# Query tiles in pairs and one written sequence, from the last linear head to the end

## Chip, cores, metric

One core of one Trainium2 chip runs the whole program in one launch. The metric is device time in microseconds (us). A kernel's time is the median of its runs.

## What is computed

One transformer block over 512 tokens of width 1024, all in float32. A wide input projection feeds two mixers: four heads of gated linear attention, in both directions, and eight heads of ordinary attention with low-rank queries and keys (64 plain and 32 rotated dimensions a head, values of 128). The two are mixed by sigmoid gates, projected by `w_out`, and an MLP of width 4096 follows.

```python
def mla_branch(cq, ckv, kr, positions, g_q, w_uq, g_kv, w_ukv):
    q = (rmsnorm(cq, g_q) @ w_uq).reshape(B, S, H, MLA_QK_HEAD)
    ...
    def attend(qblk):
        s = jnp.einsum('bhqd,bhkd->bhqk', qblk, kt).astype(jnp.float32)
        p = jax.nn.softmax(s, axis=-1)
        return jnp.einsum('bhqk,bhkv->bhqv', p.astype(vt.dtype), vt)
...
    merged = jax.nn.sigmoid(z_ma) * y_gla + jax.nn.sigmoid(z_mb) * y_mla
    h = h + merged @ w_out[l]
    m = rmsnorm(h, g_mlp[l])
    h = h + jnp.square(jax.nn.relu(m @ w_ff1[l])) @ w_ff2[l]
    return rmsnorm(h, g_final)
```

## The kernel before

**Products.** A float32 product is made of three matmuls in the chip's rounded format (fp32r): every operand is split into a high part and a low remainder, and `mm3` (L87 to L90) multiplies high by high, high by low, low by high. So behind each value that TensorE makes stand two more operations: a copy on ScalarE that rounds it (the tile whose name ends in `h`, L93) and a subtraction that keeps the remainder (`l`, L94), on VectorE or GpSimd. Transpositions go through TensorE in plain float32.

**Stages, by the time of the trace.** The input projection and most of the linear heads fill the time to about 255 us. From 255 to 290 us the last linear head (h = 3) is computed among the first queries and keys of the attention. From 290 to 374 us the attention's eight heads run, each over four tiles of 128 queries; from 374 to 413 us the output projection (a product of quarters in the manner of Strassen, `wox`, `wow`, `woz` being its banks); then four pairs of MLP phases to 722 us, whose steps are set by a table of due times, and `last_rows`, which norms and stores the last rows.

**The attention's loop (L1369 to L1453).** One turn of the loop scores one query tile: `att_scores` multiplies queries by keys (`s`, one PSUM bank), VectorE takes the row's maximum (`top`), ScalarE the exponential and its sum (`e`). Every second turn `att_normalise` divides two tiles by their sums, one on ScalarE and one on VectorE. Three turns later `att_flip` transposes one tile's four key blocks into a bank (`tp`) and splits them (`pT`). Six turns later `att_values` multiplies values by two flipped tiles, so that a head's values are two runs of twelve matmuls 256 columns wide (`av`). `merge` gates the result (`tb` on VectorE, `mx` and `my` on GpSimd, L1153). The sums of quarters `yo` and `zo`, the splits `gao`, `ghyo`, `glyo`, and the loads for `w_out` are strewn between the turns. GpSimd also issues the transfers that add their source onto a tile that is already loaded (L980, L1626; the loaded tiles are called `w`, in the orders `w2_..`).

**What sets the order.** A scheduler places the instructions of TensorE, ScalarE and VectorE in this stretch, held at some points by `goes_behind` (one instruction after another on the same engine). `in_program_order` fixes an engine to the order in which the code is written: GpSimd from the attention on, the other compute engines from the output projection on, SyncE (which issues the plain loads) from the MLP's steps on. An engine takes its instructions in the order of its queue.

**The end.** `last_rows` (L1745) sums the last products into rows 2 and 3 of tokens: `out_mean` (L1717) and `out_gained` (L1720, the gain times the row) on GpSimd, `out_square` on ScalarE, the two halves of row 3 added on VectorE (L1754, `gend0` and `gend1`), `out_rstd` (a power, L1730) on GpSimd, then one scaled product for each half of a row (L1734 on VectorE, L1738 on ScalarE) and the store.

Of the kernel before, what the change touches and what calls it, by code (L numbers as in the profile page):

```python
# [18 lines left out]
P = 128  # L19
# [35 lines left out]

@with_exitstack
def tile_block(ctx: ExitStack, tc: tile.TileContext, t, out: bass.AP):
    nc = tc.nc
# [76 lines left out]
    make_identity(nc, ident)  # L135
# [887 lines left out]
    def up_units(pr):  # L1023
# [29 lines left out]
        qs = [u4(f"q{pr}{i}") for i in range(2)]  # L1053
# [5 lines left out]
        if apart:  # L1059
            for i in range(2):  # L1060
                split_scaled(qs[i][0:64, 0, :], qs[i][0:64, 1, :], accq[i * 64 : i * 64 + 64, :], QK_SCALE)
        else:
            split_scaled(qs[0][:, 0, :], qs[0][:, 1, :], accq, QK_SCALE)
            nc.sync.dma_start(raw(qs[1][0:64]), raw(qs[0][64:128]))
            rotary_rows(0)
# [29 lines left out]
    def att_scores(head, qt):  # L1095
# [4 lines left out]
        mm3(acc, q[d, 0, tok], q[d, 1, tok], kb[d, 0, :], kb[d, 1, :], True, True)  # L1100
        top = sm("top", 1)
        nc.vector.tensor_reduce(top, acc, axis=AX.X, op=ALU.max, negate=True)  # L1102
        e = u2(f"e{head}{qt}")
        if qt % 2 == 0:
            tots[head] = sm("tot", 2)
# [10 lines left out]
    def att_flip(head, qt):  # L1116
        e = probs.pop((head, qt))
        if qt % 2 == 0:
            pTs[head, qt // 2] = [u4(f"pT{head}{qt}{x}", F32R, (P, NT, 256)) for x in range(2)]
        tp = ps("at", f"tp{head}{qt}")  # L1120
        for k in range(NT):
            nc.tensor.transpose(tp[:, k * P : (k + 1) * P], e[:, k * P : (k + 1) * P], ident)  # L1122
        hi, lo = pTs[head, qt // 2]
        c = slice((qt % 2) * P, (qt % 2 + 1) * P)
        split(hi[:, :, c], lo[:, :, c], tp.rearrange("p (k q) -> p k q", k=NT))

    def att_values(head, half):
        if half == 0:
            avs[head] = ps("mm", f"av{head}")
        acc = avs[head]  # L1130
        hi, lo = pTs.pop((head, half))
        _, _, vs, c = heads[head]
        for k in range(NT):
# [3 lines left out]
        if head < MH - 1:  # L1137
            if half == 1:
                merge(head, acc, (0, 1))
        else:  # L1140
            merge(head, acc, (half,))
# [167 lines left out]

    h = GH - 1  # L1310
# [27 lines left out]
    first_units = traced()  # L1338
# [3 lines left out]
    first_units = first_units, traced()  # L1342
    at = traced()
    zb = proj_run(w_b, xT)
    last_gate = at, traced()
    g2.append(gated(zb, "b7")[1])
    in_program_order(fixed, SPLITTERS)
    in_program_order(ordered, PE_ONLY)
    in_program_order(pooled, (mybir.EngineType.Pool,))
# [14 lines left out]
    at = traced()  # L1364
    next(units)
    goes_behind((at, traced()), first_units, SPLITTERS[:1])
    attending = traced()
    sums_of, flipping, span = {}, {}, {}
    for n in range(4 * MH + LAG_C - 1):  # L1369
        if n % 2 == 0 and 2 <= n <= 4 * MH:  # L1370
            att_normalise((n - 2) // 4, (n - 2) % 4)
        scored = traced()
        if n < 4 * MH:
            att_scores(n // 4, n % 4)
            if n - 2 in flipping:
                goes_behind((scored, traced()), flipping[n - 2], SPLITTERS)
        scored = scored, traced()
        if n == 0:
            goes_behind(scored, last_gate, PE_ONLY)
        if n == 3:  # L1380
            span["fourth"] = scored
        if 2 <= n % 8 < 7:
            at = traced()
# [3 lines left out]
            if n < 4:  # L1387
                goes_behind((at, traced()), scored, PE_ONLY)
        if n in (6, 14):
            units = up_units(n // 8 + 2)  # L1390
            at = traced()
            next(units)
            if n == 6:
                goes_behind((at, traced()), span["fourth"], SPLITTERS[:1])
        b = n - LAG_B
        if n == 30:
            xs_ = wo_accs[1] = [ps("mm", f"wox{rb}") for rb in range(2)]
            at = traced()
            wo_product(1, ps_=(0,))
            begun = at, traced()  # L1400
            goes_behind(begun, scored, PE_ONLY)
        if 0 <= b < 4 * MH:
            flips = traced()
            att_flip(b // 4, b % 4)
            flipping[n] = flips, traced()
            if n == 30:
                goes_behind(flipping[n], begun, PE_ONLY)

        if n == 20:
            load_onto(B11, B12, w_out)  # L1410
        extra = traced()
# [8 lines left out]
        if n < 4 * MH:  # L1420
            goes_behind((extra, traced()), scored, SPLITTERS[:1])
# [7 lines left out]
        if n == 17:  # L1429
            at = traced()  # L1430
            load_wo(B21, B22)
            span["sums"] = at, traced()
# [6 lines left out]
        if c >= 0 and c % 2 == 1:  # L1439
            valued = traced()  # L1440
            att_values(c // 4, (c % 4) // 2)
            valued = valued, traced()
        if n == 35:
            at = traced()
            split_first(wo_left[2], merged[2][0], "o2")
            goes_behind((at, traced()), valued, SPLITTERS[1:])
# [298 lines left out]
    def last_rows(ph):  # L1745

        begun = traced()
# [10 lines left out]
        for i in (2, 3):  # L1758
            out_first(i)
        out_gained(2)  # L1760
        out_mean(2)
# [8 lines left out]
        out_mean(3)  # L1770
# [3 lines left out]
        out_store(1)  # L1774
        p = hparts[3]
        nc.vector.scalar_tensor_tensor(p[:, 2:3], p[:, 1:2], 1.0 / D, p[:, 2:3], op0=ALU.mult, op1=ALU.add)
        last_part(1)
# [8 lines left out]
        in_program_order(begun)  # L1786

    begun = traced()  # L1790
# [8 lines left out]
    att_values(MH - 1, 1)  # L1799
# [8 lines left out]
    at = traced()  # L1808
# [190 lines left out]
```

## Time and profile before

| | |
|---|---|
| median of 3 runs | 738.93 us (738.71 to 739.01) |
| the profiled run | 739.02 us |
| its span in the trace | 737.3 us |
| granted TensorE clock | 0.998 of full speed |
| matmuls and transpositions | 4226 |
| VectorE instructions | 861 |
| ScalarE instructions | 809 |
| GpSimd instructions | 284 |

The span is what the trace covers from the first to the last instruction; 1.72 us of the run lie outside it. Busy shares are means over the whole span, so the stretch that the change touches is read from windows of 20 us. Matmuls overlap, so the cost of one is the distance from its start to the next one's start, not its length in the trace.

### The profile page before, as it was taken

How to read it: one execution, taken by the hardware profiler on the slowest of the kernel's cores; microseconds unless marked ns; L12 is line 12 of the kernel's file. 1: busy time of each engine (PE TensorE's matmuls, PEld its weight loads, DVE VectorE, ACT ScalarE, POOL GpSimd, SP SyncE). 2: the span in 40 equal slices, each digit the busy share in tenths (PEclk: the TensorE clock that was granted, in tenths of full speed). 3: DMA queues.
4: the chain of work that ended last, by engine and by line, in shares of the span. 5: the costliest groups of instructions: out<-in, count | busy, mean ns of one | idle time of the engine just before them, and what ended most of it. 6: DMA issues, size and time to landing. Idle time of an engine off the chain costs nothing.

```text
span 737.3 us, 11473 instructions
## 1 busy us (share of the span) xinstructions
PE 726.9 (99%) x4226; PEld 643.1 (87%) x4226; DVE 625.0 (85%) x861; ACT 494.2 (67%) x809; POOL 220.7 (30%) x284
## 2 busy tenths in 40 slices
PE   9999999999999999999999999999999999999995
PEld 7888888888888888899888899889988998899984
DVE  7777787889988788798898889998699869987896
ACT  7557465595696675988856879545874477537764
POOL 0732020243743724126852511200211012101215
PEclk9999999999999999999999999999999999999999
DMA  9849682431222324557978899862987088815773
GB/s 309 277 100 215 215 188 90 79 64 31 58 58 58 51 72 89 127 111 214 291 145 233 133 267 185 184 204 63 250 181 192 20 240 175 196 57 146 170 114 114
DMA packets 80520, 109.95 MB, mean 149 GB/s; under 512 B 15920, under 2 KB 34352, under 8 KB 80464
## 3 DMA queue, kind: packets, MB, share of 16 engines
q1 hardware_dynamic: 63088, 75.64, 32.9%
q0 software_dynamic: 17088, 33.30, 27.1%
q8 instruction: 33, 0.54, 0.3%
q10 hardware_dynamic: 288, 0.28, 0.1%
q14 instruction: 23, 0.19, 0.1%
HBM read 104.22 MB, written 2.10 MB: 144 GB/s over the span
## 4 chain that ended last, share of the span: by engine, by line
PE 88%; DVE 5%; issue 2%; POOL 2%; ACT 1%; DMA 1%; POOLq 0%; DVEq 0%; ACTq 0%
PE first L326 3%; PE tp L1122 2%; PE zb L88 1%; PE zb L89 1%; PE zb L90 1%; PE f2x L90 1%; PE f3x L90 1%; PE f1x L90 1%; PE f3x L89 1%; PE f2x L89 1%; PE f1x L89 1%; PE f1x L88 1%; PE f3x L88 1%; PE f2x L88 1%; PE av L89 1%
## 5 line engine op out<-in xcount | busy, mean ns | idle before, releaser
L1626 POOL DMA_DIRECT2D w<-in_w_ff x40 | 48.3, 1240 | 254.9 <-DMA w<-in_w_ff 139.3
L1102 DVE TENSOR_REDUCE top<-s 128x1 f32<-128x512 f32 x32 | 21.6, 682 | 4.9 <-PE s L90 4.7
L1107 ACT ACTIVATE e<-s,top 128x512 f32<-128x512 f32 x32 | 21.9, 687 | 3.5 <-DVE top L1102 2.6
L94 DVE TENSOR_TENSOR pT<-tp,pT 128x512 fp32r<-128x512 f32 x32 | 21.8, 682 | 2.4 <-ACT pT L93 2.0
L93 ACT ACTIVATE pT<-tp 128x512 fp32r<-128x512 f32 x32 | 19.0, 595 | 3.2 <-PE tp L1122 3.2
L1122 PE MATMUL tp<-ident,e 128*128 128x128 f32 x128 | 19.4, 274 | 0.0
L88 PE MATMUL av<-pT,v 128*128 128x256 f32 x64 | 19.1, 299 | 0.0
L90 PE MATMUL av<-pT,v 128*128 128x256 f32 x64 | 18.2, 285 | 0.0
L89 PE MATMUL av<-pT,v 128*128 128x256 f32 x64 | 18.1, 284 | 0.0
L1122 PEld LDWEIGHTS tp<-ident,e 128*128 128x128 f32 x128 | 15.2, 140 | 3.1 <-ACT e L1113 0.7
L94 POOL TENSOR_TENSOR qF<-qk,qF 128x512 fp32r<-128x512 f32 x4 | 6.6, 1641 | 37.6 <-ACT qF L93 37.6
L667 POOL DMA_DIRECT2D gvw<-in_w_in x4 | 4.8, 1230 | 38.7 <-DVE gvw L672 34.0
L667 POOL DMA_DIRECT2D zaw<-in_w_in x4 | 4.9, 1228 | 32.7 <-DVE zaw L672 28.0
L1628 DVE TENSOR_TENSOR w<-w,w 128x1024 f32<-128x1024 f32 x12 | 14.4, 1220 | 0.1
L980 POOL DMA_DIRECT2D w<-in_w_out x10 | 12.2, 1400 | 6.5 <-DVE bo60l L94 5.3
L88 PE MATMUL s<-kbuf,q 96*128 96x512 f32 x32 | 14.1, 439 | 0.0
L1153 POOL TENSOR_TENSOR mx<-tb,yg 128x256 f32<-128x256 f32 x8 | 7.7, 964 | 19.8 <-DVE tb L1150 13.9
L577 ACT ACTIVATE bds<-bd 128x512 f32<-128x512 f32 x4 | 2.4, 597 | 15.8 <-PE bd L555 15.8
L89 PE MATMUL s<-kbuf,q 96*128 96x512 f32 x32 | 12.6, 395 | 0.0
L90 PE MATMUL s<-kbuf,q 96*128 96x512 f32 x32 | 12.6, 393 | 0.0
L1113 ACT ACTIVATE e<-e,tot 128x512 f32<-128x512 f32 x16 | 11.6, 726 | 1.3 <-DVE tot L1112 1.3
L89 PEld LDWEIGHTS av<-pT,v 128*128 128x128 f32 x64 | 12.2, 191 | 0.2
(2156 smaller groups left out, 3250.4 us busy)
## 6 DMA issues: line engine op xcount, KB each, us to landing
w<-in_w_ff SPq DMA_DIRECT2D x48, 512.0 KB, 5.6
w<-in_w_ff POOLq DMA_DIRECT2D x40, 512.0 KB, 6.2
w<-in_w_out POOLq DMA_DIRECT2D x10, 512.0 KB, 8.3
grw<-in_w_in SPq DMA_DIRECT2D x8, 512.0 KB, 8.6
zaw<-in_w_in SPq DMA_DIRECT2D x8, 512.0 KB, 7.4
gvw<-in_w_in SPq DMA_DIRECT2D x8, 512.0 KB, 4.7
w<-in_w_out SPq DMA_DIRECT2D x16, 256.0 KB, 5.6
w220f<-in_w_ff SPq DMA_DIRECT2D x8, 512.0 KB, 6.2
```

The costliest lines, as they stand in the source:

```text
L88: nc.tensor.matmul(acc, lh, rh, start=start, stop=False, skip_group_check=onto)
L89: nc.tensor.matmul(acc, lh, rl, start=False, stop=False, skip_group_check=onto)
L90: nc.tensor.matmul(acc, ll, rh, start=False, stop=stop, skip_group_check=onto)
L93: nc.scalar.activation(hi, src, AF.Copy)
L94: rest.tensor_tensor(lo, src, raw(hi), op=ALU.subtract)
L326: nc.tensor.matmul(f_accs[i], a[:, i * P : (i + 1) * P], b, start=k == 0 and x == 0, stop=k == KD - 1 and x == 2)
L980: nc.gpsimd.dma_start(d, rows.rearrange("(k t p) w -> p t k w", t=2, p=P)[:, x // 2], accum_op=ALU.add)
L1102: nc.vector.tensor_reduce(top, acc, axis=AX.X, op=ALU.max, negate=True)
L1107: nc.scalar.activation(e, acc, AF.Exp, bias=top, accum_out=tot[:, qt % 2 : qt % 2 + 1])
L1122: nc.tensor.transpose(tp[:, k * P : (k + 1) * P], e[:, k * P : (k + 1) * P], ident)
L1626: nc.gpsimd.dma_start(d, self.source(src, g), accum_op=ALU.add)
L1628: nc.vector.tensor_tensor(d, d, self.tiles(src)[g], op=ALU.add)
```

## The change

**One written sequence.** `nc` is wrapped. From `nc.hold()` on, ahead of the last linear head's scores, every call on an engine is put aside under the engine's letter (P TensorE, A ScalarE, D VectorE, G GpSimd, S SyncE) and the name of the tile that it writes. `nc.emit(SEQUENCE)`, behind the output projection, issues them in the order of a string. Then `in_program_order(written)` fixes all five engines to it, through the MLP to the end. The `goes_behind` calls are gone. In the orders of the changed kernel all these instructions therefore have the wrapper's line, L76, or L90 behind it, and the tile's name tells them apart.

**Query tiles in pairs.** `att_flip` takes two query tiles at once and two key blocks of each, so that a bank holds two key blocks by 256 queries, and `pT` holds all 512 queries of a head. `att_values` runs once for a head over 512 columns (head 7 keeps two halves of 256). Queries are kept as two tiles, high and low, so each transfer of rotated rows (`ro` to `q`) becomes two of half the size.

**Last rows.** GpSimd takes both means ahead of row 2's gain, and VectorE adds `gend1` ahead of the mean term of row 3.

```diff
+    def emit(self, sequence):
+        held, self.held = self.held, None
+        for entry in sequence.split():
+            name, _, count = entry.partition("*")
+            for _ in range(int(count or 1)):
+                what, args, options = held[name].pop(0)
+                what(*args, **options)
...
-                nc.sync.dma_start(raw(qs[i][at : at + HALF]), raw(ro[x][h : h + HALF]))
+                for y in range(2):
+                    nc.sync.dma_start(raw(qs[i][y][at : at + HALF]), raw(ro[x][h : h + HALF, y]))
...
-    def att_flip(head, qt):
-        e = probs.pop((head, qt))
...
+    def att_flip(head, half):
+        if half == 0:
+            pTs[head] = [[u4(f"pT{head}{x}{k}") for k in range(2)] for x in range(2)]
+        es = [probs.pop((head, 2 * half + i)) for i in range(2)]
+        cols = slice(half * HT, (half + 1) * HT)
+        for g, (hi, lo) in enumerate(zip(*pTs[head])):
+            tp = ps("at", f"tp{head}{half}{g}")
+            for i, e in enumerate(es):
+                for k in range(2):
+                    at = k * HT + i * P
+                    nc.tensor.transpose(tp[:, at : at + P], e[:, (2 * g + k) * P : (2 * g + k + 1) * P], ident)
+            split(hi[:, :, cols], lo[:, :, cols], tp.rearrange("p (k q) -> p k q", k=2))
...
-            mm3(acc[:, half * 256 : (half + 1) * 256], vt[:, 0, k % 2, c], vt[:, 1, k % 2, c],
-                hi[:, k, :], lo[:, k, :], k == 0, k == NT - 1)
+            mm3(avs[head][:, cols], vt[:, 0, k % 2, c], vt[:, 1, k % 2, c],
+                his[k // 2][:, k % 2, cols], los[k // 2][:, k % 2, cols], k == 0, k == NT - 1)
...
-        if c >= 0 and c % 2 == 1:
-            valued = traced()
-            att_values(c // 4, (c % 4) // 2)
+        if c >= 0 and (c % 4 == 3 or c == 4 * MH - 3):
+            att_values(c // 4, (0, 1) if c // 4 < MH - 1 else (0,))
...
+    nc.hold()
+    written = traced()
     h = GH - 1
...
+        out_mean(2)
+        out_mean(3)
         out_gained(2)
-        out_mean(2)
...
-        out_mean(3)
         out_gained(3)
...
+        last_part(1)
         p = hparts[3]
         nc.vector.scalar_tensor_tensor(p[:, 2:3], p[:, 1:2], 1.0 / D, p[:, 2:3], op0=ALU.mult, op1=ALU.add)
-        last_part(1)
...
+    SEQUENCE = """
+        S:wr0f*2 S:zb6f S:wr0f A:sin A:qF D:cqc2 S:wr1f A:wr0h A:zb6h G:wr0l P:y15*4 P:y14*4 S:wq0f P:ckvss*4
...
+    nc.emit(SEQUENCE)
...
-    in_program_order(begun, PE_ONLY + SPLITTERS)
-    in_program_order(stepped, SP_ONLY)
-    in_program_order(attending, (mybir.EngineType.Pool,))
     last_rows(g3)
+    in_program_order(written)
```

Three places show how the orders stand. The first is TensorE at the values of head 3, in the middle of the attention. Before, its second half (`pT320` and `pT321` are the high and the low part of query tiles 2 and 3, `v10` the values) comes behind one transposition:

```order
L1122 MATMUL tp42_766_3710<-ident_61,e42_735_3571 128x128 x4
L88 MATMUL av3_749_3630<-pT320_726_3530,v10_612_3071 128x256
L89 MATMUL av3_749_3630<-pT321_727_3531,v10_612_3071 128x256
L90 MATMUL av3_749_3630<-pT320_726_3530,v10_612_3071 128x256
L88 MATMUL av3_749_3630<-pT320_726_3530,v10_612_3071 128x256
L89 MATMUL av3_749_3630<-pT321_727_3531,v10_612_3071 128x256
L90 MATMUL av3_749_3630<-pT320_726_3530,v10_612_3071 128x256
L88 MATMUL av3_749_3630<-pT320_726_3530,v11_618_3102 128x256
```

After, the same stretch reads (`pT300` and `pT310` are now the high and the low part of two key blocks for all 512 queries):

```order
L76 MATMUL tp400_764_2789<-ident_61,e40_724_2749 128x128 x2
L76 MATMUL tp400_764_2789<-ident_61,e41_734_2759 128x128 x2
L76 MATMUL av3_776_2801<-pT300_726_2751,v10_613_2638 128x512
L76 MATMUL av3_776_2801<-pT310_728_2753,v10_613_2638 128x512
L76 MATMUL av3_776_2801<-pT300_726_2751,v10_613_2638 128x512 x2
L76 MATMUL av3_776_2801<-pT310_728_2753,v10_613_2638 128x512
L76 MATMUL av3_776_2801<-pT300_726_2751,v10_613_2638 128x512
L76 MATMUL av3_776_2801<-pT301_727_2752,v11_624_2649 128x512
```

A head has one run of twelve wide matmuls where it had two runs of twelve narrow ones, and the transpositions of a bank take two tiles each.

The second place is GpSimd and ScalarE at the split of `mx1`, the first two query tiles' merged columns of heads 2 and 3 (`gao1`). GpSimd before, up to the remainder of that split:

```order
L1153 TENSOR_TENSOR mx2_802_3859<-tb5_535_2687,yg5_529_2674 128x256
L1153 TENSOR_TENSOR my2_803_3860<-tb5_535_2687,yg5_529_2674 128x256
L1006 TENSOR_TENSOR yo2_831_3972<-my2_803_3860 128x256
L1007 TENSOR_TENSOR yo2_831_3972<-yo2_831_3972,mx2_802_3859 128x256
L1008 TENSOR_TENSOR zo2_832_3973<-mx2_802_3859,my2_803_3860 128x256
L1009 TENSOR_TENSOR zo2_832_3973<-mx2_802_3859,yo2_831_3972 128x256
L94 TENSOR_TENSOR gao1_840_4005<-mx1_731_3557,gao1_840_4005 128x512
```

and after, up to the sum on which that split waits (`DMA w2_..` are adding transfers of `w_out`):

```order
L76 TENSOR_TENSOR my1_739_2764<-tb2_89_429,yg2_468_2365 128x256
L76 DMA w2_21_736_2761<-in_w_out 128x2x512
L76 TENSOR_TENSOR yo0_699_2724<-my0_659_2684 128x256
L76 DMA w2_20_735_2760<-in_w_out 128x2x512
L76 TENSOR_TENSOR gao0_753_2778<-mx0_658_2683,gao0_753_2778 128x512
L76 DMA w2_11_802_2827<-in_w_out 128x2x512
L76 TENSOR_TENSOR yo0_699_2724<-yo0_699_2724,mx0_658_2683 128x256
L76 TENSOR_TENSOR mx1_738_2763<-tb2_89_429,yg2_468_2365 128x256
L76 TENSOR_TENSOR my1_739_2764<-tb3_95_465,yg3_470_2372 128x256
L76 TENSOR_TENSOR yo1_777_2802<-my1_739_2764 128x256
L76 TENSOR_TENSOR mx1_738_2763<-tb3_95_465,yg3_470_2372 128x256
```

ScalarE before, up to the rounding of that split:

```order
L1107 ACTIVATE e71_827_3946,tot_821_3927<-s71_825_3940,top_826_3944 128x512
L93 ACTIVATE pT620_828_3948<-tp62_830_3950 128x4x128
L1107 ACTIVATE e72_835_3987,tot_836_3988<-s72_833_3981,top_834_3985 128x512
L1113 ACTIVATE e70_820_3926<-e70_820_3926,tot_821_3927 128x512
L93 ACTIVATE pT620_828_3948<-tp63_839_3998 128x4x128
L93 ACTIVATE gao1_840_4005<-mx1_731_3557 128x512
```

and after, around it:

```order
L76 ACTIVATE e50_756_2781<-e50_756_2781,tot50_757_2782 128x512
L76 ACTIVATE bo50h_882_2907<-w2_00_720_2745 128x1024
L76 ACTIVATE gdo0_904_2929<-my1_739_2764 128x256
L76 ACTIVATE gao1_848_2873<-mx1_738_2763 128x512
L76 ACTIVATE e61_807_2832,tot60_794_2819<-s61_805_2830,top61_806_2831 128x512
L76 ACTIVATE e60_793_2818,tot60_794_2819<-s60_791_2816,top60_792_2817 128x512
```

The split has moved from among the transpositions of heads 6 and 7 to between heads 5 and 6: behind it on ScalarE stand the exponentials of head 6's tiles 1 and 0, and ahead of the sum for it on GpSimd stand three adding transfers.

The third place is VectorE in `last_rows`, before:

```order
L1734 SCALAR_TENSOR_TENSOR ms0_1370_7609<-h0_861_4109,hp0_1369_7608,gfin_1322_7364 128x512
L1754 TENSOR_TENSOR h3_864_4115<-gend0_1374_7643,h3_864_4115 128x256
L1727 SCALAR_TENSOR_TENSOR hp2_1376_7657<-hp2_1376_7657 128x1
L1734 SCALAR_TENSOR_TENSOR ms1_1372_7612<-h1_862_4111,hp1_1371_7611,gfin_1322_7364 128x512
L1776 SCALAR_TENSOR_TENSOR hp3_1378_7660<-hp3_1378_7660 128x1
L1754 TENSOR_TENSOR h3_864_4115<-gend1_1375_7644,h3_864_4115 128x256
L1734 SCALAR_TENSOR_TENSOR ms2_1377_7658<-h2_863_4113,hp2_1376_7657,gfin_1322_7364 128x512
L1727 SCALAR_TENSOR_TENSOR hp3_1378_7660<-hp3_1378_7660 128x1
L1734 SCALAR_TENSOR_TENSOR ms3_1379_7661<-h3_864_4115,hp3_1378_7660,gfin_1322_7364 128x512
```

and after:

```order
L90 SCALAR_TENSOR_TENSOR ms0_1378_7551<-h0_869_2894,hp0_1377_7550,gfin_1330_7306 128x512
L90 TENSOR_TENSOR h3_872_2897<-gend0_1382_7585,h3_872_2897 128x256
L90 SCALAR_TENSOR_TENSOR hp2_1384_7599<-hp2_1384_7599 128x1
L90 SCALAR_TENSOR_TENSOR ms1_1380_7554<-h1_870_2895,hp1_1379_7553,gfin_1330_7306 128x512
L90 TENSOR_TENSOR h3_872_2897<-gend1_1383_7586,h3_872_2897 128x256
L90 SCALAR_TENSOR_TENSOR hp3_1386_7602<-hp3_1386_7602 128x1
L90 SCALAR_TENSOR_TENSOR ms2_1385_7600<-h2_871_2896,hp2_1384_7599,gfin_1330_7306 128x512
L90 SCALAR_TENSOR_TENSOR hp3_1386_7602<-hp3_1386_7602 128x1
L90 SCALAR_TENSOR_TENSOR ms3_1387_7603<-h3_872_2897,hp3_1386_7602,gfin_1330_7306 128x512
```

The addition of `gend1` and the first of the two terms of `hp3` have changed places.

More of the change, by code (lines that the diff above doesn't have):

```diff
@@ L134, in tile_block @@
     ident = one([P, P], F32, "ident")
-    make_identity(nc, ident)
+    make_identity(nc.nc, ident)
     after = one([P, P], F32, "after")
@@ L1060, in up_units @@
             for i in range(2):
-                split_scaled(qs[i][0:64, 0, :], qs[i][0:64, 1, :], accq[i * 64 : i * 64 + 64, :], QK_SCALE)
+                split_scaled(qs[i][0][0:64], qs[i][1][0:64], accq[i * 64 : i * 64 + 64, :], QK_SCALE)
         else:
-            split_scaled(qs[0][:, 0, :], qs[0][:, 1, :], accq, QK_SCALE)
-            nc.sync.dma_start(raw(qs[1][0:64]), raw(qs[0][64:128]))
+            split_scaled(*qs[0], accq, QK_SCALE)
+            for y in range(2):
+                nc.sync.dma_start(raw(qs[1][y][0:64]), raw(qs[0][y][64:128]))
             rotary_rows(0)
@@ L1807, in tile_block @@
     wo_right[5].append(split_part(B11, 1, "bo5"))
-    at = traced()
     f0.load(B11)
-    goes_behind((at, traced()), span["sums"], SP_ONLY)
     for rb in range(2):
```

167 lines of the change are left out of this document (98 added, 69 removed).

## The prediction

> **What bounds the kernel now.** I read the page's busy shares first, then the windows of 20 us over the changed stretch, then the timeline of single engines there, and the chain that ended last for the end of the program.
>
> ```profile
> span 737.3 us, 11473 instructions
> PE 726.9 (99%) x4226; PEld 643.1 (87%) x4226; DVE 625.0 (85%) x861; ACT 494.2 (67%) x809; POOL 220.7 (30%) x284
> ...
> 280.00:300.00 20.00, 20.00 (x106) 16.98 (x106) 15.02 (x25) 13.32 (x29) 5.31 (x8) 1.00 0.42 106
> 300.00:320.00 20.00, 20.00 (x135) 18.01 (x134) 17.36 (x33) 17.64 (x40) 4.88 (x7) 1.00 0.49 114
> 320.00:340.00 20.00, 20.00 (x136) 18.04 (x135) 17.43 (x31) 16.50 (x40) 10.50 (x14) 1.00 0.61 158
> 340.00:360.00 20.00, 20.00 (x146) 18.31 (x146) 18.03 (x33) 16.52 (x37) 15.01 (x15) 1.00 0.98 257
> 360.00:380.00 20.00, 20.00 (x129) 17.55 (x128) 17.84 (x28) 14.75 (x28) 13.79 (x15) 1.00 0.70 174
> ```
>
> The columns of the windows are the window, its length, then busy time on PE, PEld, DVE, ACT and POOL, the granted clock, the DMA share and GB/s. TensorE is busy 20.00 of 20.00 us in each, at clock 1.00. So TensorE bounds the attention, and a new order cannot gain there by filling its gaps: there are none to speak of. A gain must come from less TensorE work or from the end, behind TensorE's last matmul. A loss can come from any new wait of TensorE, and the engines that feed it have 2 to 3 us of every 20 to spare (DVE 17.36 to 18.03, ACT up to 17.64).
>
> **The change part by part: TensorE's content.** A busy PE says nothing of how much work there is, so I take distances from start to start.
>
> ```profile
> 249.15 0.39 PE L88 MATMUL zb<-xT,zb4h 128*128 128x512 f32 x1
> ...
> 254.38 0.39 PE L90 MATMUL zb<-xT,zb4l 128*128 128x512 f32 x1
> 254.60 0.49 PE L555 MATMUL bd<-qkb 128*128 128x128 f32 x3
> ...
> 306.94 0.28 PE L88 MATMUL av<-pT,v 128*128 128x256 f32 x1
> ...
> 307.66 0.60 PE L1122 MATMUL tp<-ident,e 128*128 128x128 f32 x4
> 308.01 0.36 PE L88 MATMUL av<-pT,v 128*128 128x256 f32 x1
> 308.21 0.29 PE L89 MATMUL av<-pT,v 128*128 128x256 f32 x1
> 308.34 0.28 PE L90 MATMUL av<-pT,v 128*128 128x256 f32 x1
> ```
>
> From 249.15 to 254.60 stand 24 matmuls of 512 columns: 0.227 us each. From 306.94 to 307.66 stand 6 of 256: 0.120 us each. Four transpositions take 0.35 us. The first matmul behind them (308.01 to 308.21) takes 0.20 us, 0.08 more than its like: the way from plain float32 back to the rounded format costs that much each time.
>
> Heads 0 to 6 had 7 x 24 = 168 narrow matmuls, 168 x 0.120 = 20.16 us, and get 7 x 12 = 84 wide ones, 84 x 0.227 = 19.07 us: 1.09 us less. The transpositions are as many as before, but the written order puts more of their groups side by side: TensorE goes back from a transposition to a product 32 times in the order before and 24 times after, so 8 x 0.08 = 0.64 us less. All other products are the same in number and shape. Together TensorE has 1.73 us less to do, and being the bound it gives all of it.
>
> The Trainium skill's page "TensorE: Matmul & The Clock Gate", section "Back-to-back issue gap", gives the warm distance as N / 2.4 plus 2.5 ns; by that two narrow ones (218 ns) would cost only 2.5 ns more than a wide one, 0.2 us in all instead of 1.09. The trace differs (240 against 227 ns), and I go by the trace.
>
> **New waits.** I laid out the written queues with the distances above and looked where TensorE would arrive ahead of its input. Most places have over 0.7 us to spare; some eight have 0.2 to 0.6. The one I can price best is the score `s70`, which needs the bank that the exponential `e61` leaves. On ScalarE `e61` now stands behind `gao1`, which waits for GpSimd's second sum `mx1`, behind three adding transfers.
>
> ```profile
> 341.48 0.62 ACT L93 ACTIVATE gao<-mx 128x512 fp32r<-128x512 f32 x1
> ...
> 343.70 0.68 ACT L1107 ACTIVATE e<-s,top 128x512 f32<-128x512 f32 x1
> 344.27 0.20 ACT L1107 ACTIVATION_READ_ACCUMULATOR e<-s,top 128x1 f32 x1
> ...
> 348.08 0.67 DVE L94 TENSOR_TENSOR pT<-tp,pT 128x512 fp32r<-128x512 f32 x1
> 348.68 0.67 DVE L1150 SCALAR_TENSOR_TENSOR tb<-tb,av 128x512 f32<-128x512 f32 x1
> ...
> 342.18 1.29 POOL L94 TENSOR_TENSOR gao<-mx,gao 128x512 fp32r<-128x512 f32 x1 [3.71 <-DMA bo21f<-in_w_out]
> 343.41 2.53 POOL L980 DMA_DIRECT2D w<-in_w_out  x2
> ...
> 350.12 0.74 POOL L1153 TENSOR_TENSOR my<-tb,yg 128x256 f32<-128x256 f32 x1
> 350.93 0.74 POOL L1006 TENSOR_TENSOR yo<-my 128x256 f32<-128x256 f32 x1
> ...
> L1153 POOL TENSOR_TENSOR mx<-tb,yg 128x256 f32<-128x256 f32 x8 | 7.7, 964 | 19.8 <-DVE tb L1150 13.9
> w<-in_w_out SPq DMA_DIRECT2D x16, 256.0 KB, 5.6
> ...
> q<-ro SPq DMA_DIRECT2D x10, 64.0 KB, 2.4
> ```
>
> TensorE, from `av3`'s last matmul to `s70`: three groups of transpositions (1.05), nine matmuls of 512 (2.04) and one way back (0.08), four more of 512 (0.91), twelve of 256 (1.44): 5.5 us. The other way round: the last matmul's end (0.17 past its distance), `tb3` 0.67, three sums on GpSimd at 0.74, `gao1` 0.62, `e61` 0.88: 4.6 us. That leaves 0.9 us, if GpSimd is free when `tb3` is done. Its queue from the first `my1` on, which waits for `av2`: three issues at 1.27 (2.53 for two), four sums at 0.74, one remainder at 1.29, in all 8.1 us; TensorE needs 7.7 us from `av2` to `av3`. So 0.4 us of the 0.9 are gone, and 0.5 is left. With the mean of the sums beside other work, 964 ns (the row L1153), five of them on this way take 1.1 us more, and `s70` is 0.6 us late. So this place costs between nothing and 0.6 us; I take 0.2. If one of the three adding transfers still waits for its loaded tile, as GpSimd stood 3.71 us for a load ahead of 342.18, it costs 3.71 - 0.5 = 3.2 us. The other seven narrow places are a chain of two or three operations each, and slip by some 0.1 us of each operation: none to 1 us together, since a stall at one place pushes TensorE back for all the later ones. I take 0.3. New waits: 0.5 us, bounds 0 and 1.6.
>
> **What hides the rest.** ScalarE's and VectorE's instructions keep their number; the splits `pT` keep their 512 columns, written in two runs of 256 instead of four of 128, which I cost at nothing: the subtraction of `pT` on VectorE took 0.67 us in four runs (348.08), and no row shows fewer and longer runs to be slower. Halving the transfers `ro` to `q` adds issues on SyncE's queue; the larger ones landed 2.4 us after issue (the last row above), and in the written order I find at least 2 us between landing and use for all of them.
>
> **The end.** Behind TensorE's last matmul the chain runs through VectorE and GpSimd.
>
> ```profile
> 728.32 0.28 PE L90 MATMUL gend<-g341h,f3l 128*128 128x256 f32 x1
> ...
> 727.35 0.75 DVE L1734 SCALAR_TENSOR_TENSOR ms<-h,hp,gfin 128x512 f32<-128x512 f32 x1 [0.33 <-POOL hp L1730]
> ...
> 728.42 0.75 DVE L1734 SCALAR_TENSOR_TENSOR ms<-h,hp,gfin 128x512 f32<-128x512 f32 x1
> 729.88 0.16 DVE L1776 SCALAR_TENSOR_TENSOR hp<-hp 128x1 f32<-128x1 f32 x1 [0.71 <-POOL hp L1717]
> 729.96 0.42 DVE L1754 TENSOR_TENSOR h<-gend,h 128x256 f32<-128x256 f32 x1
> 730.29 1.45 DVE L1734 SCALAR_TENSOR_TENSOR ms<-h,hp,gfin 128x512 f32<-128x512 f32 x1
> 731.66 0.15 DVE L1727 SCALAR_TENSOR_TENSOR hp<-hp 128x1 f32<-128x1 f32 x1
> 732.47 0.75 DVE L1734 SCALAR_TENSOR_TENSOR ms<-h,hp,gfin 128x512 f32<-128x512 f32 x1 [0.66 <-POOL hp L1730]
> ...
> 728.58 0.99 POOL L1730 TENSOR_TENSOR hp<-hp,mhalf 128x1 f32<-128x1 f32 x1 [0.74 <-DVE hp L1727]
> 729.66 0.19 POOL L1717 TENSOR_SCALAR hp<-hp 128x1 f32<-128x1 f32 x1
> 729.93 1.26 POOL L1720 TENSOR_TENSOR ms<-h,gfin 128x512 f32<-128x512 f32 x1
> 731.89 0.55 POOL L1730 TENSOR_TENSOR hp<-hp,mhalf 128x1 f32<-128x1 f32 x1 [0.69 <-DVE hp L1727]
> ```
>
> TensorE is done at 728.60, but VectorE adds `gend1` at 729.96, since the mean term of row 3 ahead of it waits for GpSimd's mean at 729.66. With the two exchanged and the mean taken early, the addition follows `ms1` at about 729.15 (728.42 + 0.75) and ends by 729.55. GpSimd's power of row 2 ends at about 729.55 (728.58 + 0.99), so `ms2` runs from 729.6 to 730.35, or to 731.05 if it takes 1.45 again beside GpSimd's row 3 gain; the last mean term (0.1), the power (0.55) and its wait (0.2) put `ms3` at 731.2 or 731.9 instead of 732.47. The gain is 1.3 or 0.6; I take the middle, 1.0. Only the part where both engines read at once decides between them.
>
> On 1.45 against 0.75, the Trainium skill's page "SBUF — State Buffer", section "SBUF: two separate sides", has VectorE with two SBUF inputs and GpSimd exclude one another for a whole instruction, whichever starts first; the 1.45 beside the 1.26 agrees.
>
> **Rivals.**
> (1) One load is late: at the place of `s70` an adding transfer waits 3.71 us as in the row at 342.18. For it speaks that these loads land 5.6 us after issue and that the DMA share is 0.98 in the window 340 to 360; against it, that the written order issues the three loads some turns earlier. Then -1.73 - 1.0 + 3.2 = +0.5: 739.4 us, no difference to be measured.
> (2) Slower: the same mechanism twice. GpSimd has further adding transfers ahead of the second halves of `yo1` and `zo1` and of `glyo0`, and ScalarE again has exponentials behind the roundings of those. Queues that follow a list cannot let a ready instruction pass, and DVE with 18.03 of 20 us has no room to catch up. Two such waits: -2.7 + 6.4 = +3.7, 742.6 us. It decides from 4.2 us of new waits on (2.7 saved, and 1.5 that can be measured).
> (3) Widening saves nothing. The 1.09 goes, as it would if what a narrow matmul costs more were hidden elsewhere: -2.25 + 1.09 = -1.2, 737.8 us. The rows at 306.94 speak against it. The skill's rule above would come close to this, 737.6 us.
> (4) The end gives nothing, because GpSimd's power stays last: -2.25 + 1.0, 737.7 us. Against it stands that the row at 729.88 waited for nothing but the mean.
>
> **How the numbers follow.** The sum is -1.73 + 0.5 - 1.0 = -2.2 us against the profiled run's 739.02 us (span 737.3 and 1.72 outside it), 736.8 us; the median of the runs, 738.93 us, is 0.1 lower, so 736.7 us. What a measurement of this kernel can tell from no change is about 0.2%, 1.5 us: faster is below 737.45, slower above 740.41. The forecast has 0.66; its own range goes from 735.9 (no new waits, 1.3 at the end: 738.93 - 3.03) to 737.4, where it meets no change (1.5 us of new waits beside 1.3 at the end come to 737.4). Rivals (3) and (4) have 0.06 together and rival (1) 0.12, all within the 0.2%: 0.18. Rival (2) has 0.16. The range reaches over rival (1), 739.4, with 0.3 for the spread of its wait, and leaves rival (2) out; below, it takes another 0.4 for the rounding of the distances (0.002 us on 168 matmuls is 0.3) and of the end: 735.5 to 739.7.
>
> **What would show it.** In the trace after, 84 `av` matmuls of 512 columns and 24 of 256; TensorE's last matmul 1.2 us earlier (1.73 less 0.5), ending at about 727.4; no idle time of PE over 0.6 us between 255 and 413; `e61` on ScalarE by the time that `uv31` ends on PE; and the last scaled product on VectorE 2.9 us, not 3.9, behind the last matmul's end. I am wrong if GpSimd's issues for `w_out` show a wait on a load ahead of the sums `mx1`, with PE idle ahead of `s70`; or if PE's last matmul ends later than 728.3 in a trace without idle time on PE, which would put the content wrong.

## The result and the profile after

The changed kernel takes 740.34 us (740.0 to 741.22), against 738.71 us (738.47 to 739.45) before, 17 runs each. The ratio is 1.0021, with a 95% interval from 1.0014 to 1.0029: 1.6 us slower, where 2.2 us faster was forecast. The profiled run took 740.25 us with a span of 738.5.

The page after, its span, busy shares and the grouped row of VectorE's normalisations (16 of them; before, they took 477 to 1176 ns each, 504 in the middle):

```profile
span 738.5 us, 11335 instructions
PE 726.3 (98%) x4142; PEld 637.3 (86%) x4142; DVE 625.2 (85%) x861; ACT 494.7 (67%) x809; POOL 218.3 (30%) x284
...
L76 DVE TENSOR_SCALAR e<-e,tot 128x512 f32<-128x512 f32 x16 | 12.7, 797 | 0.0
```

The windows after (columns as above). The two in which TensorE is no longer full are 280 to 300 and 360 to 380:

```profile
280.00:300.00 20.00, 19.90 (x110) 16.67 (x109) 10.88 (x20) 13.12 (x35) 5.78 (x10) 1.00 0.71 188
...
360.00:380.00 20.00, 18.36 (x103) 15.53 (x102) 17.73 (x25) 13.84 (x27) 13.62 (x16) 1.00 0.70 181
```

The waits of TensorE name one place:

```profile
PE tp L76 <- DVE e L76: 1.6, 1, 1.6
```

In the timelines it is a transposition of `e73` (head 7's fourth query tile), which waits for VectorE's normalisation of that tile (`e` in the rows below). TensorE, VectorE and GpSimd there:

```profile
373.99 0.38 PE L76 MATMUL tp<-ident,e 128*128 128x128 f32 x2
376.02 0.44 PE L76 MATMUL tp<-ident,e 128*128 128x128 f32 x2 [1.64 <-DVE e L76]
```

```profile
371.56 0.69 DVE L76 SCALAR_TENSOR_TENSOR tb<-tb,av 128x512 f32<-128x512 f32 x1 [0.15 <-PE av L76]
372.17 3.79 DVE L76 TENSOR_SCALAR e<-e,tot 128x512 f32<-128x512 f32 x1
```

```profile
371.36 1.16 POOL L76 TENSOR_TENSOR yo<-yo,mx 128x256 f32<-128x256 f32 x1
372.33 0.89 POOL L76 TENSOR_TENSOR mx<-tb,yg 128x256 f32<-128x256 f32 x1
373.02 1.43 POOL L76 TENSOR_TENSOR glyo<-yo,ghyo 128x512 fp32r<-128x512 f32 x1
374.27 1.40 POOL L76 TENSOR_TENSOR glzo<-zo,ghzo 128x512 fp32r<-128x512 f32 x1
```

An operation that takes 0.48 us alone takes 3.79. It starts while GpSimd works, and ends 0.3 us after the last of four GpSimd operations that follow each other without a gap (374.27 + 1.40 = 375.67, against 375.96).

The second loss is at the first scores. VectorE stood 8.52 us at the head of its queue, waiting for a statistic of GpSimd; behind it stood the keys that TensorE needed. VectorE, the weight loads, and TensorE:

```profile
288.09 0.48 DVE L76 SCALAR_TENSOR_TENSOR grb<-gla3o,gla3ss,grb 128x256 f32<-128x256 f32 x1 [8.52 <-POOL gla3ss L76]
288.61 0.69 DVE L76 TENSOR_TENSOR kbuf<-uk,kbuf 64x512 fp32r<-64x512 f32 x1
```

```profile
290.69 0.30 PEld L76 LDWEIGHTS s<-kbuf,q 96*128 96x128 f32 x2 [0.48 <-DVE kbuf L76]
291.48 0.53 PEld L76 LDWEIGHTS s<-kbuf,q 96*128 96x128 f32 x3 [0.49 <-DVE grc L76]
```

```profile
290.25 2.20 PE L76 MATMUL s<-kbuf,q 96*128 96x512 f32 x6
292.30 0.62 PE L76 MATMUL uk<-ckvhl,wk1h 128*128 128x512 f32 x2
```

Six matmuls of 512 columns take 2.05 us, 0.69 more than 6 x 0.227.

The third is the end. TensorE's last matmul, VectorE's scaled products with the added halves, and GpSimd:

```profile
729.34 0.28 PE L90 MATMUL gend<-g341h,f3l 128*128 128x256 f32 x1
```

```profile
727.98 1.85 DVE L90 SCALAR_TENSOR_TENSOR ms<-h,hp,gfin 128x512 f32<-128x512 f32 x1
...
730.82 0.41 DVE L90 TENSOR_TENSOR h<-gend,h 128x256 f32<-128x256 f32 x1
...
731.34 1.74 DVE L90 SCALAR_TENSOR_TENSOR ms<-h,hp,gfin 128x512 f32<-128x512 f32 x1
...
733.81 0.75 DVE L90 SCALAR_TENSOR_TENSOR ms<-h,hp,gfin 128x512 f32<-128x512 f32 x1 [0.66 <-POOL hp L90]
```

```profile
726.27 1.08 POOL L90 TENSOR_TENSOR hp<-hp,mhalf 128x1 f32<-128x1 f32 x2
...
727.98 1.30 POOL L90 TENSOR_TENSOR ms<-h,gfin 128x512 f32<-128x512 f32 x1
```

GpSimd's gain of row 2 and VectorE's first scaled product start together at 727.98, and the product takes 1.85 instead of 0.75. From the start of TensorE's last matmul to the start of the last product it was 732.47 - 728.32 = 4.15 us before, and is 4.47 now.

Both traces are set side by side from the first matmul of `zb4` (249.15 before, 248.52 after), since TensorE's instructions ahead of it are the same. From there to the start of the last matmul it is 479.17 us before and 480.82 after: TensorE's part is 1.65 us longer, and what follows it 0.18 (9.16 against 8.98 to the end of the span). In the traces of all the kernels here `zb4` starts anywhere from 248.34 to 249.62 us, behind the same instructions of TensorE. So a difference of medians of 1 us or less is firm only where these distances in the traces show it too.

### The profile page after: what moved, and what is told of

Same layout as the page of the kernel before. It is cut to its first block, busy times and chain, and to the rows that moved or that the text cites. A ratio compares the mean times of both kernels' runs of the same rounds, so it can differ in the third digit from the quotient of the medians.

```text
span 738.5 us, 11335 instructions
## 1 busy us (share of the span) xinstructions
PE 726.3 (98%) x4142; PEld 637.3 (86%) x4142; DVE 625.2 (85%) x861; ACT 494.7 (67%) x809; POOL 218.3 (30%) x284
## 4 chain that ended last, share of the span: by engine, by line
PE 96%; DVE 2%; issue 1%; POOL 0%; SPq 0%; DMA 0%; POOLq 0%; DVEq 0%
PE f3x L90 3%; PE f2x L90 3%; PE f1x L90 3%; PE f0x L90 3%; PE s L76 3%; PE first L90 3%; PE g2x L90 3%; PE g1x L90 3%; PE g0x L90 3%; PE gvx L90 3%; PE zax L90 3%; PE grx L90 3%; PE av L76 3%; PE wox L76 3%; PE gk L90 2%; PE cq L90 2%
## 5 line engine op out<-in xcount | busy, mean ns | idle before, releaser
L90 POOL DMA_DIRECT2D w<-in_w_ff x34 | 40.9, 1204 | 247.9 <-DMA w<-in_w_ff 137.7
L76 PE MATMUL s<-kbuf,q 96*128 96x512 f32 x96 | 27.2, 403 | 0.1
L76 PE MATMUL av<-pT,v 128*128 128x512 f32 (+1 forms) x108 | 25.5, 374 | 0.0
L76 DVE TENSOR_REDUCE top<-s 128x1 f32<-128x512 f32 x32 | 21.5, 682 | 4.0 <-PE s L76 4.0
L76 ACT ACTIVATE e<-s,top 128x512 f32<-128x512 f32 x32 | 22.0, 688 | 3.7 <-DVE top L76 2.3
L76 DVE TENSOR_TENSOR pT<-tp,pT 128x512 fp32r<-128x512 f32 x32 | 21.6, 684 | 3.0 <-ACT pT L76 2.6
L76 ACT ACTIVATE pT<-tp 128x512 fp32r<-128x512 f32 x32 | 18.5, 601 | 7.3 <-PE tp L76 6.7
L76 PEld LDWEIGHTS av<-pT,v 128*128 128x128 f32 x108 | 18.5, 189 | 3.3
L76 PEld LDWEIGHTS s<-kbuf,q 96*128 96x128 f32 x96 | 16.9, 189 | 4.5 <-DVE grc L76 0.5
L76 PE MATMUL tp<-ident,e 128*128 128x128 f32 x128 | 18.2, 274 | 1.6 <-DVE e L76 1.6
L76 PEld LDWEIGHTS tp<-ident,e 128*128 128x128 f32 x128 | 15.1, 140 | 4.8 <-DVE e L76 1.9
L90 POOL DMA_DIRECT2D gvw<-in_w_in x4 | 4.8, 1230 | 38.7 <-DVE gvw L90 34.0
L76 POOL DMA_DIRECT2D w<-in_w_out x10 | 13.5, 1396 | 6.7 <-DVE bo61l L76 4.4
L90 POOL TENSOR_TENSOR qF<-qk,qF 128x512 fp32r<-128x512 f32 x3 | 5.3, 1758 | 32.8 <-ACT qF L90 32.8
L90 POOL DMA_DIRECT2D zaw<-in_w_in x4 | 4.9, 1228 | 32.7 <-DVE zaw L90 28.0
L90 DVE TENSOR_TENSOR w<-w,w 128x1024 f32<-128x1024 f32 x12 | 14.4, 1221 | 0.1
L76 DVE TENSOR_SCALAR e<-e,tot 128x512 f32<-128x512 f32 x16 | 12.7, 797 | 0.0
L76 ACT ACTIVATE e<-e,tot 128x512 f32<-128x512 f32 x16 | 11.6, 730 | 0.5 <-DVE tot L76 0.5
L76 POOL TENSOR_TENSOR my<-tb,yg 128x256 f32<-128x256 f32 x8 | 6.7, 836 | 15.6 <-DVE tb L76 15.6
L90 ACT ACTIVATE f3h<-f3a 128x512 fp32r<-128x512 f32 x10 | 6.1, 621 | 6.2 <-DVE f3a L90 6.2
L90 ACT ACTIVATE f0h<-f0a 128x512 fp32r<-128x512 f32 x10 | 6.1, 620 | 6.2 <-DVE f0a L90 6.2
```

Of the source, the lines that this page charges most:

```text
L76: what(*args, **options)
L90: return what(*args, **options)
```

## The experiments

All times are medians; `before` was 738.63 beside the first four kernels, 738.87 beside the next four and 738.66 beside the last four.

**Normalising ahead of gating (e1).** One exchange in the written order:

```diff
-D:tb6 A:ghzo0 P:wow0*3 D:e73
+D:e73 D:tb6 A:ghzo0 P:wow0*3
```

> The changed kernel with one exchange in the written order: VectorE normalises head 7's fourth tile (e73) ahead of gating head 6's values (tb6), not behind. Theory (GpSimd's elementwise work holds VectorE's SBUF-to-SBUF work): GpSimd's sums of tb6 then have no input yet, e73 takes under 1.3 us instead of 3.79, the wait of TensorE of 1.64 us is gone, and the time falls by 1.5 to 1.9 us, to about 738.6. Rival (VectorE's queue is simply too full here, whatever GpSimd does): e73 ends at most 0.6 us earlier, and the time falls by 0 to 0.6.

Measured 738.32 us, 2.0 less than the changed kernel, ratio to before 0.9996 (0.9987 to 1.0005). VectorE, then GpSimd, in this run:

```profile
371.18 1.36 DVE L76 TENSOR_SCALAR e<-e,tot 128x512 f32<-128x512 f32 x1
372.47 0.67 DVE L76 SCALAR_TENSOR_TENSOR tb<-tb,av 128x512 f32<-128x512 f32 x1
```

```profile
371.09 1.16 POOL L76 TENSOR_TENSOR yo<-yo,mx 128x256 f32<-128x256 f32 x1
373.22 1.66 POOL L76 TENSOR_TENSOR mx<-tb,yg 128x256 f32<-128x256 f32 x1 [0.97 <-DVE tb L76]
```

`e73` ends 0.29 us after `yo` (372.54 against 372.25), because GpSimd then waits for `tb6`. Its 1.36 us are a little more than the forecast allowed. TensorE's wait is gone. From `zb4` to the last matmul it is 479.02 us, 1.80 less than in the changed kernel. The theory holds here; but an exchange moves the start too, so e5 takes it from the other side.

**GpSimd lighter at that place (e5).** The queue around `e73` is left alone, and the last two of the four GpSimd operations go to VectorE, behind `bo21l`:

```diff
-D:bo21l A:ghyo2 P:wox1*3 G:glyo1
+D:bo21l D:glyo1 A:ghyo2 P:wox1*3
...
-A:gao3 G:glzo0
+A:gao3 D:glzo0
```

> The changed kernel with GpSimd's last two remainders in the stretch around 373 us (glyo1, glzo0) given to VectorE, behind bo21l; the queue around e73 stays. Theory (GpSimd's run of elementwise work without a gap holds e73): e73 starts as before at about 372.2 and is let go when GpSimd's sum mx3 ends, so it takes 0.9 to 1.5 us instead of 3.79, TensorE's 1.64 us wait goes, and the time falls by 1.4 to 1.9 us, to about 738.6. Rival (e73 is slow from its place on VectorE or from transfers into SBUF): e73 stays over 3 us and the time is as before or, with 1.2 us more on VectorE, up to 0.5 higher.

Measured 738.46 us, 1.9 less, with 1.3 us more work on VectorE. VectorE and GpSimd:

```profile
372.05 1.34 DVE L76 TENSOR_SCALAR e<-e,tot 128x512 f32<-128x512 f32 x1
```

```profile
371.23 1.18 POOL L76 TENSOR_TENSOR yo<-yo,mx 128x256 f32<-128x256 f32 x1
372.21 0.88 POOL L76 TENSOR_TENSOR mx<-tb,yg 128x256 f32<-128x256 f32 x1
```

The operation ahead of `e73` on VectorE is the same, and it starts at the same time: 1.34 us instead of 3.79, ending 0.30 after `mx` (373.39 against 373.09). The rival, a full queue or transfers, is out. At this place GpSimd's run of operations held VectorE.

**The statistic behind the keys (e2).**

```diff
-G:gla3ss G:wk1l D:grb A:wk1h D:kbuf1 A:kbuf0 G:wk1l D:q001 D:kbuf0 D:grc A:tb5 D:grc
+G:gla3ss G:wk1l A:wk1h D:kbuf1 A:kbuf0 G:wk1l D:q001 D:kbuf0 D:grb D:grc A:tb5 D:grc
```

> The changed kernel with the one instruction on which VectorE stood 8.52 us (grb, waiting for GpSimd's gla3ss) put behind the splits kbuf1, q001 and kbuf0. Theory (the head of VectorE's queue delays the first scores): the 0.69 us that TensorE loses around 290.3 goes, and the time falls by 0.5 to 0.7 us, to about 739.7. Rival (the later narrow places eat what an earlier place gives): the wait goes, but waits behind it grow, and the time falls by less than 0.2.

Measured 739.74 us, 0.6 less than the changed kernel, ratio to before 1.0014 (1.0005 to 1.0023). TensorE in this run:

```profile
290.59 1.55 PE L76 MATMUL s<-kbuf,q 96*128 96x512 f32 x6
291.98 0.63 PE L76 MATMUL uk<-ckvhl,wk1h 128*128 128x512 f32 x2
```

From their start to the next product the six matmuls take 1.39 us, against 6 x 0.227 = 1.36. From `zb4` to the last matmul it is 480.09 us, 0.73 less than in the changed kernel, so the gain is not eaten by the later places.

**GpSimd's gain ahead of the powers (e3).**

```diff
-        out_mean(2)
-        out_mean(3)
         out_gained(2)
+        out_pow(0)
+        out_pow(1)
+        out_mean(2)
+        out_mean(3)
```

(`out_pow` is the power of `out_rstd`, taken out of it; for rows 0 and 1 only VectorE's term stays at the old place.)

> The changed kernel with GpSimd's gain of row 2 put ahead of the powers of rows 0 and 1, as before; VectorE keeps the changed order. Theory (the gain collides with VectorE's first scaled product, which took 1.85 instead of 0.75): that product takes under 1.0 us, the last scaled product starts 3.1 to 3.5 us behind the last matmul's start instead of 4.47, and the time falls by 1.0 to 1.4, to about 739.1. Rival (GpSimd's chain of powers and row 3's gain sets the end anyway): 4.2 us or more, and the time falls by less than 0.3.

Measured 739.27 us, 1.07 less than the changed kernel. VectorE's first and last scaled product, and the last matmul:

```profile
727.93 0.75 DVE L90 SCALAR_TENSOR_TENSOR ms<-h,hp,gfin 128x512 f32<-128x512 f32 x1
...
732.68 0.75 DVE L90 SCALAR_TENSOR_TENSOR ms<-h,hp,gfin 128x512 f32<-128x512 f32 x1 [0.66 <-POOL hp L90]
```

```profile
729.31 0.28 PE L90 MATMUL gend<-g341h,f3l 128*128 128x256 f32 x1
```

3.37 us from matmul to product, where the changed kernel has 4.47 and the kernel before 4.15.

**The last rows alone, in the kernel before (e9, e10).** e9 takes the changed kernel's last rows with their order, e10 also puts the gain ahead of the powers.

> The kernel before with nothing changed but the last rows, in the order of the changed kernel on VectorE and GpSimd. Theory (the gain of row 2, now behind the powers, collides with VectorE's first scaled product): 0.2 to 0.5 us slower than before, with the last scaled product starting about 4.5 us behind the last matmul's start, not 4.15. Rival, the prediction's step (the exchange on VectorE saves its wait): 0.6 to 1.3 us faster.

> The kernel before with the last rows of the changed kernel, but GpSimd's gain of row 2 ahead of the powers of rows 0 and 1. Theory (the exchange on VectorE is worth what the prediction gave it, once GpSimd's gain is out of the way): 0.6 to 1.0 us faster than before, the last product at 3.4 us behind the last matmul's start. Rival (the gain of row 3, which still meets the product of row 2, sets the end): less than 0.3 faster.

e9 measured 738.79 us, ratio 1.0003 (0.9994 to 1.0012): the sum of a loss and a gain, and by itself not told from zero. Its trace has the collision again: the first scaled product takes 1.84 us, and the last one comes 4.43 us behind the last matmul (732.49 against 728.06).

e10 measured 737.85 us, ratio 0.9990 (0.9981 to 0.9999), 0.8 less than before; the last product comes 3.36 us behind (732.09 against 728.73). Its first product and that of row 2:

```profile
727.35 0.75 DVE L1739 SCALAR_TENSOR_TENSOR ms<-h,hp,gfin 128x512 f32<-128x512 f32 x1
...
729.61 1.75 DVE L1739 SCALAR_TENSOR_TENSOR ms<-h,hp,gfin 128x512 f32<-128x512 f32 x1
```

So the new last rows are worth 0.8 us, and the change lost it by moving GpSimd's gain behind the powers, which costs 1.1 (e3). VectorE's exchange is not all of the 0.8. Before, the first product waited 0.33 us for its power. In e10 the powers stand ahead of the mean of row 2, that wait is gone, and the product starts 1.38 us ahead of the last matmul's start instead of 0.97. By this the powers give about 0.4 of the 0.8, and the exchange with the early mean of row 3 the rest; no run takes the two apart.

**The three edits together (e6, and e12 on another chip).**

> The three edits of the first runs together: e73 ahead of tb6, grb behind three splits, and the gain of row 2 ahead of the powers. Theory (three separate causes at three places, one after another on TensorE's path): the gains of 2.0, 0.6 and 1.1 us add up, 736.7 us against 740.3 for the changed kernel and 738.6 before. Rival (they share one cover): two of them give most, and the sum is under 2.7, over 737.6.

> The kernel with the three edits once more, on the same chip as the three others, as the base for the transpositions put apart. Theory: 2.0 to 2.3 us faster than before, as the first time.

Measured 736.67 us, ratio to before 0.9972 (0.9961 to 0.9982), and 736.77, ratio 0.9976 (0.9967 to 0.9985). It beats both kernels: 2.2 and 1.9 us under the kernel before, 3.7 under the changed one, as 2.0 + 0.6 + 1.1 add up to.

**Narrow values again (e4, e7).** Twice as many matmuls of 256 columns at the places of the wide ones, in the changed kernel (e4) and in the one with the three edits (e7):

```diff
-            mm3(avs[head][:, cols], ...)
+            for n, (v_, p_) in enumerate(((0, his), (0, los), (1, his))):
+                for x in halves_:
+                    nc.tensor.matmul(avs[head][:, w], vt[:, v_, k % 2, c], p_[k // 2][:, k % 2, w], ...)
```

> The changed kernel with the values of heads 0 to 6 multiplied in twice as many matmuls of 256 columns, at the same places; all else as changed. Theory (the widening saves 1.09 us of TensorE's work, which other waits then hid): the time rises by 0.7 to 1.1 us, to about 741.2, and some small waits shrink. Rival (widening saves nothing, since narrow matmuls cost no more in the stream): within 0.3 of the changed kernel.

> The kernel with the three edits, and the values of heads 0 to 6 multiplied in matmuls of 256 columns again, two where one of 512 stands. Theory (the widening saves 1.09 us of TensorE's work, and no large wait is left to hide it): 1.1 us slower than the kernel with the three edits. Rival (half of it or more comes back as small waits, since VectorE and ScalarE are nearly full in the attention): slower by 0.5 or less.

e4 measured 739.08 us, 1.26 less than the changed kernel, against both expectations. (e4 begins the accumulation of a bank twice, once for each half, and its values come out wrong; e7 begins it once. The number and the widths of the matmuls are the same.) More work on TensorE and less time: the trace shows why.

```profile
372.09 0.69 DVE L76 SCALAR_TENSOR_TENSOR tb<-tb,av 128x512 f32<-128x512 f32 x1 [0.32 <-PE av L76]
372.70 0.50 DVE L76 TENSOR_SCALAR e<-e,tot 128x512 f32<-128x512 f32 x1
```

```profile
371.73 1.17 POOL L76 TENSOR_TENSOR yo<-yo,mx 128x256 f32<-128x256 f32 x1
372.86 0.93 POOL L76 TENSOR_TENSOR mx<-tb,yg 128x256 f32<-128x256 f32 x1
```

With TensorE later, `tb6` came later, and `e73` began at 372.70, half a microsecond later than in the changed kernel. GpSimd's `yo` was then nearly over: its row ends at 372.90, and such rows overlap by up to 0.2 us (372.52 against 372.33 in the changed kernel). `e73` took 0.50 us. Half a microsecond of timing decided over 1.8.

e7, where that place is mended, measured 737.76 us against 736.67. So the widening is worth 1.09 us by the medians, as forecast, but their intervals overlap (ratios to before 0.9985, 0.9976 to 0.9994, and 0.9972, 0.9961 to 0.9982). The traces carry it: from `zb4` to the last matmul TensorE takes 478.95 us in e7 and 478.04 in e6, 0.91 more. The match of the medians to the hundredth is chance.

**Gain of row 3 early (e8).** On top of the three edits, GpSimd takes row 3's gain right behind the means, and VectorE adds `gend0` ahead of its first product.

```diff
         out_mean(3)
+        out_gained(3)
         add_rows(2, 0, acc)
+        last_part(0)
         out_left(0)
...
-        last_part(0)
         out_rstd(2)
         out_square(3, cols[0])
-        out_gained(3)
```

> The three edits, and in the last rows GpSimd's gain of row 3 right behind the two means, with VectorE adding gend0 ahead of its first scaled product. Theory (VectorE's product and GpSimd's gain exclude one another, so that the gain is best placed where VectorE reads PSUM): the product of row 2 takes under 1.0 us instead of 1.75, the last product starts 2.4 to 3.0 us behind the last matmul's start instead of 3.37, and the time is 0.4 to 0.9 us below the kernel with the three edits, about 736.1. Rival (the gain then holds VectorE's first product instead): no faster than the three edits.

Measured 737.24 us, 0.6 more than 736.67: the last product comes 3.84 us behind the last matmul (730.72 against 726.88), in e6 3.30. VectorE and GpSimd:

```profile
729.24 0.75 DVE L90 SCALAR_TENSOR_TENSOR ms<-h,hp,gfin 128x512 f32<-128x512 f32 x1 [0.52 <-POOL hp L90]
730.72 0.75 DVE L90 SCALAR_TENSOR_TENSOR ms<-h,hp,gfin 128x512 f32<-128x512 f32 x1 [0.66 <-POOL hp L90]
```

```profile
726.97 1.73 POOL L90 TENSOR_TENSOR ms<-h,gfin 128x512 f32<-128x512 f32 x1
728.66 0.54 POOL L90 TENSOR_TENSOR hp<-hp,mhalf 128x1 f32<-128x1 f32 x1
```

The product of row 2 takes 0.75, as expected, but GpSimd's power of row 2 now stands behind the longer gain, and the product waits for it until 729.24. The collision was turned into a wait; neither expectation had named it, though the rival's time, no faster, came true.

**Transpositions put apart (e11).** One matmul of the product that follows is put between neighbouring groups of transpositions, at nine places, for instance:

```diff
-P:tp101*4 P:tp100*4 A:e31 P:s20*3
+P:tp101*4 P:s20 P:tp100*4 A:e31 P:s20*2
```

> The kernel with the three edits, and one matmul of the product that follows put between transpositions of different banks that stood side by side, at nine places. The prediction's step (each way back from plain float32 to the rounded format costs 0.08 us, so groups side by side save it): 0.7 us slower than the kernel with the three edits. Theory now (each group of four pays its 0.08 wherever it stands, also behind another group): within 0.2 of it.

Measured 736.58 us, against 736.77 with the three edits on the same chip. The way back to the rounded format is made nine times more, and from `zb4` to the last matmul TensorE takes 478.19 us against 478.07 (e12): 0.12 more, where nine times 0.08 would be 0.7.

## Why the prediction was wrong, point by point

The sum had -2.2 us and the runs +1.6. The step that failed most is the price of the new waits, 0.5 us and at most 1.6: two waits cost 2.5 together. The two other steps that failed are the ways back (-0.64, of which e11 leaves some 0.1) and the end (-1.0, measured +0.3).

**Widening, -1.09: right**, 0.91 by the traces of e7 and e6, which answers rival (3). The formula of the Trainium skill's page "TensorE: Matmul & The Clock Gate", section "Back-to-back issue gap", is given there for a matmul by itself. Rival (3) took it for a stream.

**Fewer ways back, -0.64: wrong.** The step read the 0.08 us on the first product behind transpositions and gave it to the change of format. In the trace after, eight transpositions take 0.80 us and four take 0.36 before the next product starts:

```profile
310.94 1.04 PE L76 MATMUL tp<-ident,e 128*128 128x128 f32 x8
311.74 0.94 PE L76 MATMUL s<-kbuf,q 96*128 96x512 f32 x3
...
315.98 0.60 PE L76 MATMUL tp<-ident,e 128*128 128x128 f32 x4
316.34 0.36 PE L76 MATMUL uv<-wk2h,ckvhl 128*128 128x256 f32 x1
```

0.80 is 2 x 0.36 and 0.08: a group pays its 0.08 behind another group as well as ahead of a product, and e11 agrees. All rows quoted beforehand had one group between products, and could not tell the two readings apart. What in the group costs it is not shown.

**New waits, +0.5 within 0 and 1.6: wrong, 2.5.** The place priced in most detail, `s70`, cost nothing: the score starts at 352.63, twelve matmuls of 0.12 us behind the start of `uv31`.

```profile
351.21 0.28 PE L76 MATMUL uv<-wk3h,ckvhl 128*128 128x256 f32 x1
...
352.63 0.63 PE L76 MATMUL s<-kbuf,q 96*128 96x512 f32 x2
```

From 249 to 413 us no wait of GpSimd is put down to a load, so rivals (1) and (2) fell with their mechanism, though the sign of (2) came true. The two that cost stood elsewhere: `e73` 1.80 (e1) and the keys behind `grb` 0.73 (e2, from 480.82 to 480.09 on TensorE). The prediction names neither place. The first was hidden by the method: I took each operation at its usual length, 0.48 us for a normalisation, with some 0.1 for slips, and asked only which input came last. Before, one normalisation had taken 1.18 us already (346.38), beside a remainder of GpSimd's (345.57 to 347.26), and what GpSimd does in that time is part of the price. For the second, a ready instruction stood behind a waiting one at the head of a written queue: I had this as a rival for the sums on GpSimd, not for VectorE's keys.

**The end, -1.0: wrong in sign, +0.3.** The step that failed is "the mean taken early" being free: taking it and the powers first moved GpSimd's gain, which had ended at 726.40, to the time of VectorE's first product. The powers come first because `in_program_order(written)` now holds GpSimd through `last_rows`. Before, GpSimd's fixed order ended ahead of `last_rows`, and its gain stood ahead of the powers. I allowed for such a collision at row 2's product and not at row 0's, where the change put a new one. Without that move the last rows are worth 0.8 (e10), inside the 0.6 to 1.3, but partly by luck: row 2's product took 1.75 us and not the 1.45 at most, and about half of the 0.8 comes from the powers ahead of the mean, which the sum does not have.

The Trainium skill's page "SBUF — State Buffer", section "SBUF: two separate sides", which I named for the collision at row 2, speaks for the one at row 0 too: it lets an operation wait for one instruction of the other engine. It speaks for `e73`, which has one input in SBUF beside its scale, only if that runs in a mode of VectorE that uses two ports, and no run here shows the mode. The traces agree that the two engines exclude one another: most normalisations that met GpSimd's work waited for one instruction. But `e73` waited through four.

**The sum.** On TensorE: -0.91 for the widening, +1.80 and +0.73 for the two waits, together +1.62 of the +1.65 that the traces show. So close a fit is partly chance: the three edits together took 2.78 off TensorE (480.82 to 478.04), 0.25 more than the two waits measured one by one. At the end +0.2 to +0.3. With the three places mended, TensorE takes 478.04 us from `zb4` to its last matmul, 1.13 less than before: 0.91 is the widening, and the written order by itself gave TensorE some 0.2.

## What to carry to other kernels

When an order is written out, price VectorE's work on SBUF by what GpSimd runs beside it, and look at GpSimd's longest run without a gap: a short operation waited for one instruction of it at most places here, and for all of it at one, on TensorE's path. Where a critical operation must stand near such a run, put it ahead of the one that feeds GpSimd, which costs one exchange. And before a term is taken from an excess in the timeline, look for a row that would tell two readings of it apart.

## What the runs showed of the hardware

`e73`, a VectorE operation from SBUF to SBUF, was not let in between GpSimd's elementwise instructions: it ended 0.3 us after the last of an unbroken run, of one (1.36 us in e1), two (1.34 in e5) or four (3.79 after, and again in e2 and e3). Other normalisations of the same form were let in at the first change of instruction. In the changed kernel one met the first of three that follow each other without a gap, and ended about 0.3 us after that first one (324.50 against 324.21; VectorE, then GpSimd):

```profile
323.56 0.94 DVE L76 TENSOR_SCALAR e<-e,tot 128x512 f32<-128x512 f32 x1
```

```profile
323.20 1.01 POOL L76 TENSOR_TENSOR wq3l<-wq3f,wq3h 128x384 fp32r<-128x384 f32 x1 [16.41 <-ACT wq3h L76]
324.17 0.92 POOL L76 TENSOR_TENSOR mx<-tb,yg 128x256 f32<-128x256 f32 x1
325.05 0.74 POOL L76 TENSOR_TENSOR my<-tb,yg 128x256 f32<-128x256 f32 x1
```

So an unbroken run does not hold VectorE everywhere, and why it held `e73` is open. VectorE's subtractions `pT`, which read one operand from PSUM, were never held, though many stood beside the same kind of work. All 32 in the changed kernel (shortest, median and longest in ns):

```profile
L76 DVE TENSOR_TENSOR pT<-tp,pT x32: 672/683/693, 305.4 to 380.4; 128x512 fp32r<-128x512 f32 x32
```
